# Encoder layer on one core: other slots, order and pieces for the expert weights, logits in column groups

## The chip, the cores and the metric

The kernel runs on one core of a Trainium2 chip. The metric is device time of one execution, in microseconds; the runs of the kernel before gave 1866.06, 1867.19 and 1870.11, so its median is 1867.19. A profiled execution of its own gave the trace that all rows below come from.

## The reference, cut to what matters

One encoder layer: 256 tokens of width 2048, float32. A token-mixing sub-layer (attention, a recurrent branch, gates, an output projection `w_out`) is followed by a routed mixture of 16 experts, in which each expert takes its own 32 best tokens.

```python
def expert_choice_ffn(hn, w_router, w_gate_e, w_up_e, w_down_e):
    cap = CAPACITY_FACTOR * T // N_EXPERTS                       # 32
    aff = softmax(hn @ w_router, axis=-1)                        # 256 tokens x 16 experts
    gate, idx = top_k(aff.transpose(0, 2, 1), cap)
    xe = hn[idx]                                                 # per expert 32 x 2048
    hid = silu(xe @ w_gate_e) * (xe @ w_up_e)                    # 2048 -> 1024
    ye = (hid @ w_down_e) * gate                                 # 1024 -> 2048
    return zeros.at[idx].add(ye)
...
h = h + merged @ w_out
h = h + expert_choice_ffn(rms_norm(h, ffn_norm_g), w_router, w_gate_e, w_up_e, w_down_e)
```

Every expert has three weight matrices of 8 MB, so the expert stage reads 384 MB of weights from HBM, each byte once.

## The kernel before, in words

The instructions of each engine stand in an order that a scheduler (the tile framework with a timeline simulation) chose; each engine then runs its own list in order, and waits on semaphores. DMAs are issued by SP, in order too: a DMA that has to wait holds up all that stand behind it on SP. Eight semaphores go round among SP's DMAs, and a DMA waits until the one eight places ahead has landed, so at most eight are in flight.

Stages: token mixing, to about 820 us of the trace; the output projection (`project_t`, tiles `pj_wo`), four blocks of 512 columns with eight chunks of weights each; routing; experts.

Output projection. `wsplit` (line 200) loads half a megabyte of weights into one of three buffers `raw`, splits it on ACT (`wh`) and DVE (`wl`), and PE runs 12 products on the chunk. Behind each block, PE transposes the finished columns of `h` and multiplies them with the router's weights (line 843, tile `plg`, eight products with 16 columns each); DVE adds the blocks' logits up in `lgt`.

Expert weights come in loads of 1 MB, `ew_loads`, in the order of use; `fetch` (line 171) issues the next one into a slot. There are 14 lasting slots (`NEW`, two of them in pool `ew1`, 12 in `ewa`), which are used round and round, and eight more (`NEB`, pool `ewb`), used once, in memory that becomes free when the output projection and its logits are done. `pace` (line 188) puts one load behind every third chunk (`PACE = 3`) of the last token-mixing blocks and of the output projection, until the 14 slots are full.

Routing (lines 855 to 893): softmax of the logits, then the 32 best tokens of each expert by four rounds of `max` and `match_replace` on DVE, and their places `slot`.

Experts are taken in four groups of four (`q`). `gather(k4)` (line 918) makes a quarter of the gathered, transposed tokens `xe` by products with a one-hot matrix `ohr` (PE, tile `pxe`, 16 records in the trace) and a multiplication on DVE. Eight steps `c` (line 928) use eight loads each (gate and up of four experts) and accumulate into four PSUM tiles `pgu`; the four experts stand in four groups of 32 columns of TensorE. Then the activation, transposes, and the down products (line 974, tile `pd`) in pieces of the 2048 output columns, given by `pieces`: two of 1024 columns, and in the last group one of 1024, one of 512 and two of 256. Behind each piece follow a copy on ACT (`ye`), products that scatter the rows back to the tokens (`poe`, line 982), an addition on DVE (`acc`), and in the last group the stores of `out`.

```python
NEW, NE1, NEB = 14, 2, 8
PACE = 3
...
for c in range(8):
    if c % 2 == 0:
        gather(c // 2)
    wt = []
    for j in range(4):
        wt += [expert_w(), expert_w()]
```

Of the kernel before, what the change touches and what calls it, by code (L numbers as in the profile page):

```python
# [8 lines left out]
F32 = mybir.dt.float32  # L9
# [9 lines left out]
T = 256  # L19
# [16 lines left out]
NEW, NE1, NEB = 14, 2, 8  # L36
PACE = 3
# [15 lines left out]
def trunk_kernel(ctx, tc, x, attn_norm_g, w_in, q_norm_g, k_norm_g, lambda_q1, lambda_k1, lambda_q2,  # L53
# [93 lines left out]
    def pieces(q):  # L147

        return ((0, 1024), (1024, 1024)) if q < 3 else ((0, 1024), (1024, 512), (1536, 256), (1792, 256))

    ew_loads = []
    for q in range(4):
        for c in range(8):
            for j in range(4):
                for src in (w_gate_e, w_up_e):
                    ew_loads.append(src[0, 4 * q + j].rearrange("(p kt) f -> p kt f", kt=KT)[:, 2 * c:2 * c + 2])
        for c0, w in pieces(q):
            n = 2048 // w
            for c in range(8 // n):
                for j in range(4):  # L160
                    ew_loads.append(w_down_e[0, 4 * q + j].rearrange("(p ft) n -> p ft n", ft=8)
                                    [:, n * c:n * c + n, c0:c0 + w])
    ew_state = dict(pools=[None, None, None], tiles=[], used=0, chunks=0)

    def slot_of(i):

        if NEW <= i < NEW + NEB:
            return 2
        return int((i if i < NEW else i - NEB) % NEW >= NE1)
# [30 lines left out]
    def wsplit(src, a, b, name):  # L200
        raw = wp.tile([128, 1024], F32, name="raw_" + name, tag="raw", bufs=3)
# [624 lines left out]
    with ExitStack() as es:  # L826
        o2 = es.enter_context(tc.tile_pool(name="out2", bufs=2, side=right))
        for blk in range(4):
# [32 lines left out]
    mx = rt_.tile([128, 6], F32, name="mx")  # L861
# [13 lines left out]
    V.tensor_copy(wk[0], paf)  # L875
    m8 = rt_.tile([16, 8], F32, name="m8")
    for i in range(4):
        a, b = wk[i % 2], wk[(i + 1) % 2]
# [9 lines left out]
    V.tensor_scalar(pos, pos, -1.0, None, op0=OP.add)  # L888
# [14 lines left out]
    with ExitStack() as es:  # L903
        ewb = tc.alloc_tile_pool(name="ewb", bufs=NEB, side=left)
        ew_state["pools"][2] = ewb
        for q in range(4):
# [11 lines left out]
            def gather(k4):  # L918
                px = mp.tile([128, 4, 128], F32, name=f"pxe{q}_{k4}", tag="x", bufs=1)
                for j in range(4):  # L920
                    kt = 4 * k4 + j
                    for t in range(2):
                        PE.matmul(px[:, j], h[:, t, kt::KT], ohr[:, t], start=t == 0, stop=t == 1)  # L923
                V.tensor_tensor(xe[k4], px,  # L924
                                fg[:, 4 * k4:4 * k4 + 4].unsqueeze(2).to_broadcast([128, 4, 128]), op=OP.mult)

            pgu = [pjp.tile([128, 512], F32, name=f"pgu{q}_{i}", tag="pj") for i in range(4)]
            for c in range(8):
                if c % 2 == 0:
                    gather(c // 2)  # L930
                wt = []
                for j in range(4):
                    wt += [expert_w(), expert_w()]
                for gu in range(2):
                    for k in range(2):
                        kt = 2 * c + k
                        for hf in range(2):
                            for j in range(4):
                                js = slice(32 * j, 32 * j + 32)
                                PE.matmul(pgu[2 * gu + hf][js], xe[kt // 4][:, kt % 4, js],  # L940
                                          wt[2 * j + gu][:, k, hf * 512:(hf + 1) * 512], start=kt == 0, stop=kt == KT - 1)
            if q == 0:
                ewb.release()
# [20 lines left out]
            for c0, cw in pieces(q):  # L964
                nw = min(cw, 512)
                nft = 2048 // cw
                pd = [misc([128, nw], f"pd{q}_{c0}_{i}") for i in range(cw // nw)]
                for c in range(8 // nft):
                    wt = [expert_w() for j in range(4)]
# [67 lines left out]
```

## Time and profile before

| what | value |
|---|---|
| median of 3 runs | 1867.19 us |
| profiled execution, its own time | 1860.5 us |
| its span, first to last instruction | 1858.7 us |
| PE busy | 1667.8 us, 90% |
| DVE, ACT, POOL busy | 700.0, 440.0, 197.0 us |
| moved by DMA | 556.48 MB, mean 299 GB/s |
| largest shares of the chain that ended last | PE 47%, DMA 38%, DVE 8% |

The busy shares are averages over stages with different limits: token mixing keeps PE, DVE and ACT busy and the DMA engines at half their time, the expert stage does the reverse. So the stage has to be read first, and the share second. "PE busy" says little in the expert stage, since a product that waits in the pipeline counts as busy.

### The profile page before, as it was taken

The numbers are of one execution on the slowest core, as the hardware profiler recorded it, in microseconds if no ns is written. First come the engines' busy times: TensorE is split into PE (matmuls) and PEld (weight loads), VectorE is DVE, ScalarE is ACT, GpSimd is POOL, SyncE is SP. The second block draws the span as 40 slices with busy tenths as digits, with TensorE's granted clock in tenths as the row PEclk, the third lists the DMA queues.
The fourth block names the chain that finished last, engine by engine and source line by source line (L and its number), as shares of the span: only waits on it lengthen the run. The fifth ranks groups of instructions, "written<-read, shape, count | busy, mean of one in ns | idle before, by whom it ended". The sixth has DMA issues, their size and how long they took to land.

```text
span 1858.7 us, 27458 instructions
## 1 busy us (share of the span) xinstructions
PE 1667.8 (90%) x11179; PEld 1024.7 (55%) x11179; DVE 700.0 (38%) x1523; ACT 440.0 (24%) x767; POOL 197.0 (11%) x304
## 2 busy tenths in 40 slices
PE   6999999999999999999799889888898888878878
PEld 5988888888997778998644222232222222211123
DVE  4687888787746778764500000000000000000000
ACT  6444444443434555444300000000000000000000
POOL 3243223333001321000000000000000000000000
PEclk9999999999999999999999999999999999999989
DMA  6545645455645666788899999999999999999997
GB/s 172 169 133 155 162 118 135 109 148 152 176 141 176 204 203 221 230 267 284 311 420 399 423 421 427 426 427 423 421 425 427 427 424 421 425 427 426 426 416 281
DMA packets 229598, 556.48 MB, mean 299 GB/s; under 512 B 40186, under 2 KB 137840, under 8 KB 196448
## 3 DMA queue, kind: packets, MB, share of 16 engines
q1 hardware_dynamic: 228896, 554.42, 79.7%
q8 instruction: 88, 1.44, 0.3%
q0 software_dynamic: 576, 0.31, 0.2%
q14 instruction: 38, 0.31, 0.0%
HBM read 543.14 MB, written 11.53 MB: 298 GB/s over the span
## 4 chain that ended last, share of the span: by engine, by line
PE 47%; DMA 38%; DVE 8%; POOL 3%; issue 2%; SPq 1%; ACT 1%; DVEq 0%; POOLq 0%; ACTq 0%
DMA w<-in_w_gate_e_dram 21%; DMA w<-in_w_down_e_dram 14%; PE pgu L940 8%; PE pd L974 2%; PE pc_gt L245 2%; PE pc_gt L247 2%; PE pc_gt L246 2%; PE pj_da L227 2%; PE pj_da L228 2%; PE pj_da L229 2%; PE pxe L923 2%; PE pc_br L245 2%; PE pc_br L247 2%; PE pc_br L246 2%; PE pj_wo L228 2%
## 5 line engine op out<-in xcount | busy, mean ns | idle before, releaser
L940 PE MATMUL pgu<-w,xe 128*32 128x512 f32 x2048 | 456.6, 607 | 64.2 <-DMA w<-in_w_gate_e_dram 33.0
L940 PEld LDWEIGHTS pgu<-w,xe 128*32 128x32 f32 x2048 | 110.9, 110 | 393.9 <-issue 232.6
L974 PE MATMUL pd<-w,hdT 128*32 128x512 f32 (+1 forms) x1088 | 246.2, 593 | 54.7 <-DMA w<-in_w_down_e_dram 53.8
L974 PEld LDWEIGHTS pd<-w,hdT 128*32 128x32 f32 x1088 | 64.7, 111 | 232.9 <-DMA w<-in_w_down_e_dram 122.1
L245 PE MATMUL pc_gt<-xh,wh_gt 128*128 128x256 f32 x512 | 148.4, 293 | 1.3 <-ACT wh_gt L207 1.3
L247 PE MATMUL pc_gt<-xh,wl_gt 128*128 128x256 f32 x512 | 142.9, 290 | 3.8 <-DVE wl_gt L208 3.5
L246 PE MATMUL pc_gt<-xl,wh_gt 128*128 128x256 f32 x512 | 144.5, 285 | 0.0
L955 ACT ACTIVATE th<-pgu 128x512 f32<-128x512 f32 x8 | 4.8, 597 | 521.4 <-PE pgu L940 521.4
L924 DVE TENSOR_TENSOR xe<-pxe,fg 128x512 f32<-128x512 f32 x16 | 11.0, 690 | 295.8 <-PE pgu L940 241.4
L245 PE MATMUL pc_rkv<-xh,wh_rkv 128*128 128x256 f32 x384 | 111.5, 293 | 2.3 <-ACT wh_rkv L207 1.7
L247 PE MATMUL pc_rkv<-xh,wl_rkv 128*128 128x256 f32 x384 | 109.3, 295 | 3.5 <-DVE wl_rkv L208 3.5
L246 PE MATMUL pc_rkv<-xl,wh_rkv 128*128 128x256 f32 x384 | 110.0, 289 | 0.0
L983 DVE TENSOR_TENSOR acc<-poe,acc 128x512 f32<-128x512 f32 (+1 forms) x26 | 16.9, 650 | 247.1 <-PE poe L982 247.0
L245 PEld LDWEIGHTS pc_gt<-xh,wh_gt 128*128 128x128 f32 x512 | 97.6, 191 | 4.6 <-ACT wh_gt L207 1.5
L956 DVE SCALAR_TENSOR_TENSOR th<-th,pgu 128x512 f32<-128x512 f32 x8 | 5.5, 687 | 249.7 <-ACT th L955 216.4
L247 PEld LDWEIGHTS pc_gt<-xh,wl_gt 128*128 128x128 f32 x512 | 95.0, 191 | 7.1 <-DVE wl_gt L208 4.6
L246 PEld LDWEIGHTS pc_gt<-xl,wh_gt 128*128 128x128 f32 x512 | 97.7, 191 | 2.0 <-issue 1.3
L208 DVE TENSOR_TENSOR wl_gt<-raw_gt,wh_gt 128x1024 fp32r<-128x1024 f32 x64 | 80.1, 1252 | 29.8 <-ACT wh_gt L207 27.7
L207 ACT CAST wh_gt<-raw_gt 128x1024 fp32r<-128x1024 f32 x64 | 66.9, 1046 | 80.4 <-PE pc_gt L246 62.6
L978 ACT COPY ye<-pd 128x512 f32<-128x512 f32 (+1 forms) x17 | 9.5, 560 | 309.7 <-PE pd L974 309.7
L228 PE MATMUL pj_da<-wl_da,xh 128*128 128x512 f32 x192 | 76.6, 399 | 1.7 <-DVE wl_da L208 1.7
L245 PEld LDWEIGHTS pc_rkv<-xh,wh_rkv 128*128 128x128 f32 x384 | 74.1, 193 | 6.0 <-ACT wh_rkv L207 2.2
(390 smaller groups left out, 2862.2 us busy)
## 6 DMA issues: line engine op xcount, KB each, us to landing
w<-in_w_gate_e_dram SPq DMA_DIRECT2D x128, 1024.0 KB, 19.5
w<-in_w_up_e_dram SPq DMA_DIRECT2D x128, 1024.0 KB, 19.5
w<-in_w_down_e_dram SPq DMA_DIRECT2D x128, 1024.0 KB, 18.1
raw_gt<-in_w_in_dram SPq DMA_DIRECT2D x64, 512.0 KB, 3.8
raw_rkv<-in_w_in_dram SPq DMA_DIRECT2D x48, 512.0 KB, 3.8
raw_da<-in_w_in_dram SPq DMA_DIRECT2D x48, 512.0 KB, 3.5
raw_wo<-in_w_out_dram SPq DMA_DIRECT2D x32, 512.0 KB, 5.6
raw_br<-in_w_branch_b_dram SPq DMA_DIRECT2D x16, 512.0 KB, 4.2
```

The costliest lines, as they stand in the source:

```text
L207: cast_ = A.copy(wh[:, :n], raw[:, :n])
L208: low_ = V.tensor_tensor(wl[:, :n], raw[:, :n], wh[:, :n].bitcast(F32), op=OP.subtract)
L227: PE.matmul(ps[t], lh[:, kt, s], wh[:, j], start=first, stop=False)
L228: PE.matmul(ps[t], lh[:, kt, s], wl[:, j], start=False, stop=False)
L229: PE.matmul(ps[t], ll[:, kt, s], wh[:, j], start=False, stop=last)
L245: PE.matmul(ps[c][:m], wh[:, j, cs], rh[:, kt], start=first, stop=False)
L246: PE.matmul(ps[c][:m], wh[:, j, cs], rl[:, kt], start=False, stop=False)
L247: PE.matmul(ps[c][:m], wl[:, j, cs], rh[:, kt], start=False, stop=last)
L923: PE.matmul(px[:, j], h[:, t, kt::KT], ohr[:, t], start=t == 0, stop=t == 1)
L940: PE.matmul(pgu[2 * gu + hf][js], xe[kt // 4][:, kt % 4, js], wt[2 * j + gu][:, k, hf * 512:(hf + 1) * 512], start=kt == 0, stop=kt == KT - 1)
L974: PE.matmul(pd[nb][js], hT[:, ft, js], wt[j][:, k, nb * nw:(nb + 1) * nw], start=ft == 0, stop=ft == 7)
L983: V.tensor_tensor(acc[:, t, cs], po, (h if q == 0 else acc)[:, t, cs], op=OP.add)
```

## The change

What it does, in the order of the program:

- Memory: the scratch for POOL's DMAs takes 2048 bytes a partition, `raw` has four buffers, `mx` is padded by 32 columns. The expert slots are 16 lasting ones and 6 + 2 that are used once, the last two in a pool of their own. In the built program all 24 slots start at multiples of 256 bytes; before, the 14 lasting ones did, and the eight others started 128 bytes past one.
- `PACE` is 2: one load behind every second chunk.
- Loads of gate and up weights: four gates, then four ups (before: gate, up, gate, up).
- Logits: per block four products, one in each group of 32 columns of TensorE, over 256 tokens, accumulated in PSUM over all blocks; at the end a copy on DVE and two products with a summing matrix `rsum`.
- Routing: two DVE instructions less (a copy, and a subtraction that moves into the constants).
- The first gather is made in two halves; the gathers of the later groups stand behind the products of the first four loads of the down stage of the group ahead (`issue_after(behind)`).
- The last 1024 columns of the last group: three chunks of the usual shape (two `ft`, 1024 columns, one expert a load), and then four loads that each hold one `ft` and 512 columns for all four experts, column half by column half; each half is scattered and stored when its two loads are used.

```diff
-NEW, NE1, NEB = 14, 2, 8
-PACE = 3
+NEW, NE1, NEB = 16, 2, (6, 2)
+PACE = 2
...
-            for j in range(4):
-                for src in (w_gate_e, w_up_e):
+            for src in (w_gate_e, w_up_e):
+                for j in range(4):
                     ew_loads.append(src[0, 4 * q + j].rearrange("(p kt) f -> p kt f", kt=KT)[:, 2 * c:2 * c + 2])
...
+            if last_piece(q, c0):
+                for nb in range(2):
+                    for ft in (6, 7):
+                        ew_loads.append(w_down_e[0, 4 * q:4 * q + 4].rearrange("e (p ft) n -> p e ft n", ft=8)
+                                        [:, :, ft, c0 + nb * 512:c0 + nb * 512 + 512])
...
-        raw = wp.tile([128, 1024], F32, name="raw_" + name, tag="raw", bufs=3)
+        raw = wp.tile([128, 1024], F32, name="raw_" + name, tag="raw", bufs=4)
...
-            pl = misc([128, 2, NE], f"plg{blk}")
-            for t in range(2):
-                for j in range(4):
-                    PE.matmul(pl[:, t], hT[:, j, t * 128:(t + 1) * 128], wr[:, blk * 4 + j], start=j == 0, stop=j == 3)
-            if blk == 0:
-                V.tensor_copy(lgt, pl)
-            else:
-                V.tensor_tensor(lgt, pl, lgt, op=OP.add)
+            for j in range(4):
+                PE.matmul(plg[32 * j:32 * j + NE], wr[:, blk * 4 + j], hT[:, j], start=blk == 0, stop=blk == 3)
+        lgs = o2.tile([128, T], F32, name="lgs", bufs=1)
+        V.tensor_copy(lgs, plg)
+        pl = misc([128, 2, NE], "pl")
+        for t in range(2):
+            PE.matmul(pl[:, t], lgs[:, t * 128:(t + 1) * 128], rsum[:, 0:NE], start=True, stop=True)
+        V.tensor_copy(lgt, pl)
...
-    V.tensor_copy(wk[0], paf)
...
-    V.tensor_scalar(pos, pos, -1.0, None, op0=OP.add)
...
-                if c % 2 == 0:
-                    gather(c // 2)
+                if q == 0 and c < 2:
+                    gather(0, c)
+                elif c % 2 == 0:
+                    with tc.issue_after(behind.ins) if q else nullcontext():
+                        gather(c // 2)
...
+                for ft in range(6 if last_piece(q, c0) else 8):
+                    if ft % 2 == 0:
+                        wt = [expert_w() for j in range(4)]
+                    for nb in range(2):
+                        mm = down(nb, ft, [w[:, ft % 2, nb * 512:(nb + 1) * 512] for w in wt])
+                    if c0 == 0 and ft == 1:
+                        behind = mm
+                for nb in range(2):
+                    if last_piece(q, c0):
+                        for ft in (6, 7):
+                            w4 = expert_w()
+                            down(nb, ft, [w4[:, j] for j in range(4)])
+                    scatter(nb)
```

Three places show how the lists of the engines change. First SP at the end of the output projection (`raw_wo` are its weights, `w` the expert loads), before:

```order
L205 DMA raw_wo_4_10745<-in_w_out_dram 128x2x512
L205 DMA raw_wo_5_10763<-in_w_out_dram 128x2x512
L179 DMA w<-in_w_gate_e_dram 128x2048
L205 DMA raw_wo_6_10784<-in_w_out_dram 128x2x512
L205 DMA raw_wo_7_10802<-in_w_out_dram 128x2x512
L179 DMA w<-in_w_gate_e_dram 128x2048
L179 DMA w<-in_w_up_e_dram 128x2048 x2
L179 DMA w<-in_w_gate_e_dram 128x2048
L179 DMA w<-in_w_up_e_dram 128x2048
```

and now:

```order
L209 DMA raw_wo_4_10746<-in_w_out_dram 128x2x512
L209 DMA raw_wo_5_10764<-in_w_out_dram 128x2x512
L183 DMA w<-in_w_up_e_dram 128x2048
L209 DMA raw_wo_6_10782<-in_w_out_dram 128x2x512
L209 DMA raw_wo_7_10800<-in_w_out_dram 128x2x512
L183 DMA w<-in_w_up_e_dram 128x2048
L183 DMA w<-in_w_gate_e_dram 128x2048 x4
L183 DMA w<-in_w_up_e_dram 128x2048 x4
```

The load behind `raw_wo_7` is the 16th now, where it was the 12th; the rows behind it are the loads into the slots that are used once. Their first waits now for the last product of the output projection (`pj_wo`) alone, and the seventh for the logits; before, the first waited for the last `plg` product, and with it all eight.

Then PE in the first group of experts, from the transposes `phd` on (`pd` are the down products, `pxe` the gathers of the next group), now:

```order
L974 MATMUL phd_1_11355<-cst,hd 128x128 x4
L982 MATMUL pd_0_0_11361<-w,hdT 32x512 x2
L982 MATMUL pd_0_1_11362<-w,hdT 32x512 x2
...
L982 MATMUL pd_0_1_11362<-w,hdT 32x512 x4
L933 MATMUL pxe_0_11602<-ohr,h 128x128 x8
...
L933 MATMUL pxe_1_11708<-ohr,h 128x128 x8
L982 MATMUL pd_0_0_11361<-w,hdT 32x512
L982 MATMUL pd_0_1_11362<-w,hdT 32x512
L933 MATMUL pxe_2_11814<-ohr,h 128x128 x8
...
L933 MATMUL pxe_3_11920<-ohr,h 128x128 x8
```

Before, three of these four gathers stood among the gate and up products of the group ahead, and none behind `phd`:

```order
L940 MATMUL pgu_1_10937<-w,xe_10935 32x512
L923 MATMUL pxe_3_11926<-ohr,h 128x128 x8
L940 MATMUL pgu_0_10936<-w,xe_10935 32x512
...
L962 MATMUL phd_1_11361<-cst,hd 128x128 x4
L974 MATMUL pd_0_0_11367<-w,hdT 32x512
L974 MATMUL pd_0_1_11368<-w,hdT 32x512
```

Last, the end of PE's list (the last 1024 columns of the last group), before:

```order
L974 MATMUL pd_1024_0_13556<-w,hdT 32x512 x32
L982 MATMUL poe_1024_0_0_13607<-ye,gT 128x512
L982 MATMUL poe_1024_0_1_13610<-ye,gT 128x512
L974 MATMUL pd_1536_0_13615<-w,hdT 32x256 x32
L982 MATMUL poe_1536_0_0_13658<-ye,gT 128x256
L982 MATMUL poe_1536_0_1_13661<-ye,gT 128x256
L974 MATMUL pd_1792_0_13666<-w,hdT 32x256 x32
L982 MATMUL poe_1792_0_0_13709<-ye,gT 128x256
L982 MATMUL poe_1792_0_1_13712<-ye,gT 128x256
```

and now:

```order
L982 MATMUL pd_1024_0_13550<-w,hdT 32x512 x8
L991 MATMUL poe_1024_0_0_13638<-ye,gT 128x512
L991 MATMUL poe_1024_0_1_13642<-ye,gT 128x512
L982 MATMUL pd_1024_1_13551<-w,hdT 32x512 x8
L991 MATMUL poe_1024_1_0_13660<-ye,gT 128x512
L991 MATMUL poe_1024_1_1_13664<-ye,gT 128x512
```

Of the 32 products that stood between two scatters eight are left; the others come earlier, as their loads land. On SP the store of the first 1024 columns, which stood ahead of the last two loads, now stands behind all of them.

## Rows read from the trace of the kernel before

**Rows 1.** The page: GB/s moved in each of 40 equal slices of the span.
```profile
GB/s 172 169 133 155 162 118 135 109 148 152 176 141 176 204 203 221 230 267 284 311 420 399 423 421 427 426 427 423 421 425 427 427 424 421 425 427 426 426 416 281
```

**Rows 2.** Windows: us, engines' busy time (instructions), PEclk, DMA share, GB/s.
```profile
824.00:910.00 86.00, 86.00 (x415) 71.87 (x414) 38.60 (x38) 37.04 (x47) 1.57 (x9) 1.00 0.84 294
910.00:915.00 5.00, 4.87 (x25) 3.63 (x24) 2.20 (x3) 1.06 (x3) 0.30 (x1) 1.00 0.71 301
915.00:920.00 5.00, 2.43 (x19) 2.00 (x17) 2.48 (x17) 2.21 (x8) 0.00 (x0) 1.00 0.31 100
920.00:935.00 15.00, 6.55 (x34) 4.72 (x38) 8.61 (x26) 0.00 (x0) 0.00 (x0) 0.54 1.01 425
950.00:990.00 40.00, 39.22 (x203) 21.28 (x202) 4.21 (x7) 0.37 (x1) 0.00 (x0) 1.00 1.01 426
995.00:1005.00 10.00, 10.00 (x64) 3.12 (x62) 0.00 (x0) 0.00 (x0) 0.00 (x0) 1.00 0.75 298
1130.00:1280.00 150.00, 131.30 (x546) 43.17 (x545) 6.02 (x10) 1.54 (x3) 0.00 (x0) 0.97 1.01 427
1290.00:1365.00 75.00, 62.19 (x252) 16.16 (x252) 3.21 (x5) 2.24 (x4) 0.00 (x0) 1.00 1.03 421
1802.00:1820.00 18.00, 13.25 (x54) 3.35 (x49) 2.77 (x4) 1.17 (x2) 0.00 (x0) 0.94 1.05 405
1844.00:1848.00 4.00, 4.00 (x27) 2.21 (x27) 0.00 (x0) 0.00 (x0) 0.00 (x0) 1.00 0.43 152
```

**Rows 3.** Timeline of SP: start, us, DMA issues (expert loads, one store).
```profile
903.62 2.30 SPq L179 DMA_DIRECT2D w<-in_w_up_e_dram  x2
917.53 0.33 SPq L179 DMA_DIRECT2D w<-in_w_gate_e_dram  x1
...
937.40 0.80 SPq L179 DMA_DIRECT2D w<-in_w_gate_e_dram  x2
...
985.27 0.38 SPq L179 DMA_DIRECT2D w<-in_w_up_e_dram  x1
1000.16 0.33 SPq L179 DMA_DIRECT2D w<-in_w_gate_e_dram  x1
...
1829.36 3.24 SPq L986 DMA_DIRECT2D out_dram<-acc  x2
```

**Rows 4.** Tile w, the expert weights: products' weight loads, and issue to landing.
```profile
L940 PEld LDWEIGHTS pgu<-w,xe x2048: 106/110/178, 933.7 to 1764.2; 128*32 128x32 f32 x187
...
DMA to landing us min/median/max: 4.5/18.8/21.1
```

**Rows 5.** Timeline of PE, end of the output projection to the first experts.
```profile
896.02 1.86 PE L843 MATMUL plg<-wr,hT 128*128 128x16 f32 x16
...
913.47 0.39 PE L229 MATMUL pj_wo<-wh_wo,ml 128*128 128x512 f32 x1
...
929.04 3.84 PE L923 MATMUL pxe<-ohr,h 128*128 128x128 f32 x16 [1.20 <-DVE ohr L913]
...
933.67 2.85 PE L940 MATMUL pgu<-w,xe 128*32 128x512 f32 x24 [0.36 <-DVE xe L924]
```

**Rows 6.** Timeline of DVE in routing: the two instructions that go.
```profile
921.22 0.41 DVE L875 COPY wk<-paf 16x256 f32<-16x256 f32 x1 [0.69 <-PE paf L872]
...
927.05 0.28 DVE L888 TENSOR_SCALAR wk<-wk 16x256 f32<-16x256 f32 x1
```

**Rows 7.** The chain that ended last, its end: start, us, what.
```profile
1800.43 3.62 PE pd L974 x20
...
1826.61 0.59 ACT ye L978
...
1829.23 11.45 PE pd L974 x64
...
1842.31 11.45 PE pd L974 x64
...
1855.42 0.42 DVE acc L983
```

More of the change, by code (lines that the diff above doesn't have):

```diff
@@ L1 @@
 import math
-from contextlib import ExitStack, contextmanager
+from contextlib import ExitStack, contextmanager, nullcontext
 import concourse.bass as bass
@@ L145, in trunk_kernel, with last_piece @@
                 V.scalar_tensor_tensor(xl[:, kt], pt[:, i], g, xh[:, kt].bitcast(F32), op0=OP.mult, op1=OP.subtract)
-    def pieces(q):
-        return ((0, 1024), (1024, 1024)) if q < 3 else ((0, 1024), (1024, 512), (1536, 256), (1792, 256))
+    def last_piece(q, c0):
+        return q == 3 and c0 > 0
     ew_loads = []
@@ L963, in trunk_kernel, with down, scatter @@
                 A.copy(hT[:, 4 * f4:4 * f4 + 4], pt)
[L964 to L969, printed above, removed]
-                    for k, nb, j in ([(k, 0, j) for j in range(4) for k in range(nft)] if nft == 8 else
-                                     [(k, nb, j) for k in range(nft) for nb in range(cw // nw) for j in range(4)]):
-                                ft = nft * c + k
-                                js = slice(32 * j, 32 * j + 32)
-                                PE.matmul(pd[nb][js], hT[:, ft, js], wt[j][:, k, nb * nw:(nb + 1) * nw],
-                                          start=ft == 0, stop=ft == 7)
-                for nb in range(cw // nw):
+            for c0 in (0, 1024):
+                pd = [misc([128, 512], f"pd{q}_{c0}_{i}") for i in range(2)]
+                def down(nb, ft, wf):
+                    for j in range(4):
+                        js = slice(32 * j, 32 * j + 32)
+                        mm = PE.matmul(pd[nb][js], hT[:, ft, js], wf[j], start=ft == 0, stop=ft == 7)
+                    return mm
+                def scatter(nb):
@@ L983, in trunk_kernel @@
                         V.tensor_tensor(acc[:, t, cs], po, (h if q == 0 else acc)[:, t, cs], op=OP.add)
-                if q == 3:
+                        if last_piece(q, c0):
+                            SP.dma_start(out[0, t * 128:(t + 1) * 128, cs], acc[:, t, cs])
+                for ft in range(6 if last_piece(q, c0) else 8):
+                    if ft % 2 == 0:
+                        wt = [expert_w() for j in range(4)]
+                    for nb in range(2):
+                        mm = down(nb, ft, [w[:, ft % 2, nb * 512:(nb + 1) * 512] for w in wt])
+                    if c0 == 0 and ft == 1:
+                        behind = mm
@@ L985, in trunk_kernel @@
+                for nb in range(2):
+                    if last_piece(q, c0):
+                        for ft in (6, 7):
+                            w4 = expert_w()
+                            down(nb, ft, [w4[:, j] for j in range(4)])
+                    scatter(nb)
+                if q == 3 and c0 == 0:
                     for t in range(2):
-                        SP.dma_start(out[0, t * 128:(t + 1) * 128, c0:c0 + cw], acc[:, t, c0:c0 + cw])
+                        SP.dma_start(out[0, t * 128:(t + 1) * 128, 0:1024], acc[:, t, 0:1024])
```

62 lines of the change are left out of this document (33 added, 29 removed).

## The prediction

> **What bounds the kernel now.** I read the page's slices first: up to slice 20 the kernel moves a good half of what it moves afterwards, and from slice 21 on 420 to 427 GB/s almost without a gap [rows 1]. So the program has two halves with different limits, and a line by line ranking over the whole span would mix them. Windows by stage come next [rows 2]. In the output projection (824 to 910 us) PE is busy for all of 86.00 us, with the DMA engines at 0.84: PE sets the time. From 920 us on the DMA share is 1.01 to 1.05, while PE has idle time (131.30 of 150 in 1130 to 1280): in the expert stage the weights set the time. One load of 1 MB (1.0486 MB) takes 1.0486/427 = 2.46 us among gate and up loads, 1.0486/421 = 2.49 us among down loads with 4 KB runs, and 1.0486/405 = 2.59 us with 2 KB runs [rows 2].
>
> A stage that DMA bounds is shortened only by starting its stream earlier, closing its gaps, making its loads quicker, or shortening what follows the last byte. The timeline of SP and the low windows give the gaps: 915 to 920 with 100 GB/s and 995 to 1005 with 298 [rows 2, 3]. In 1844 to 1848 the share is 0.43; against 1.05 at full rate, that is 1.6 us of data, so the last byte lands near 1845.6 and the span, 1858.7, ends 13.1 us later. The end of the chain shows what fills these [rows 7].
>
> **The change part by part.** The sum is made against the profiled execution's own 1860.5 us, which is 6.7 below the median of the runs; that difference is added at the end.
>
> *1. Logits.* A block's `plg` is 16 records in 1.86 us [rows 5]. Now it is four products, eight records of 256 columns. The lower bound is the weight load alone, 8 x 0.110 = 0.9 us [rows 4]; the upper is 11.45/64 = 0.179 a record of 256 columns [rows 7], so 1.4. I take 1.1: 0.75 less for each of the three blocks that stand inside dense PE work, 2.3 us in all (1.3 to 2.9). The fourth stands behind the projection's last product. That product ends at 913.47 + 0.39 = 913.9 [rows 5], and now at 911.6.
>
> *2. Start of the stream.* The first load into a once-used slot goes out at 917.53 [rows 3], because it waits for the last `plg`. In 915 to 920 the engines are nearly empty. Now it waits for the last projection product, so 911.7, and 16 loads instead of 14 are there or under way. What is late next is the first reuse of a slot. The first expert product is at 933.67, 19.8 us after the projection's last [rows 5]. Of that path go 0.41 and 0.28 on DVE [rows 6], about 0.4 by half a first gather (half of the 3.84 us, most of it beside other work), and some 0.5 is added by the copy `lgs` and the two summing products: 19.2, with 0 to 1 for the addition. The first `pgu` product is then at 930.8. The first slot came free 937.40 - 933.67 = 3.7 us after it [rows 3, 5]; now 934.5. A load on unloaded engines lands after 4.5 us [rows 4], so the 25th lands at 939.0. Before, it was the 11th after 917.53: 917.53 + 4.5 + 10 x 2.47 = 946.7 (425 GB/s). Gain 7.7, with 5 to 10 as bounds. Supply alone would give more, since the 24 loads are there by about 911.7 + 9 x 2.47 = 934, half a microsecond before the slot; so the routing path, not the stream, sets this.
>
> *3. The gap at 995 to 1005.* No load is issued between 985.27 and 1000.16 [rows 3], because three gathers of the next group stand among the gate and up products and hold the slots. The window moves 298 instead of 426 GB/s: 10 x (1 - 298/426) = 3.0 us at most, 10 x (1.01 - 0.75) = 2.6 by the share, and nothing if the pause only comes back at another place. I take 2, nearer to the row. The gathers now stand behind the first `pd` products: 4 x 3.84 = 15.4 us of PE time [rows 5], some 19 us with the products in between. In that time 19/2.49 = 8 loads land. There are 16 slots and at most eight loads in flight, so eight landings are covered; the stage then has PE time to catch up (62.19 busy of 75 in 1290 to 1365 [rows 2]). I cost it at nothing; what it costs without that cover is rival E.
>
> *4. The last 16 loads.* Before, they were eight with 2 KB runs and eight with 1 KB, and the store of `out` (1 MB) was issued at 1829.36, ahead of the last two [rows 3]. They took from about 1800.4, where the last products on the loads before them begin [rows 7], to 1845.6: 45.2 us. Now it is 12 x 2.49 + 4 x 2.59 = 40.2, and the store comes behind them: gain 5.0.
>
> The four new loads fetch four runs per partition, 8 MB apart; no row shows such a load. From below, 2.46 us each [rows 2] (0.1 less each). From above, the slowest stretch of the stream, 100 GB/s in 915 to 920, though that was starved and not slow: 10.5 each, 32 more in all. I take 2.59, the row with runs of the same size, since all loads of the trace fetch runs spread over 128 partitions and their rate moves with the size of a run by some per cent only. The Trainium skill ("DMA: Bandwidth & Descriptors", section "Latency and other measured facts") reports that rows a large power of two apart drop to 103 GB/s at 8 MiB. By that a load takes 10.2 us as an estimate, and the sum gives a loss of about 10. In these four loads 128 partitions lie as close as before and only four runs of each are far apart, so I weigh the rule as rival F.
>
> *5. The tail.* Before, two pieces of 64 `pd` records of 11.45 us each stand behind one another at the end, the last from 1842.31 to 1853.8 [rows 7]. Now four products, one copy, two `poe`, an addition and the store follow the last byte. By the gather's 3.84/16 = 0.24 for 128 columns [rows 5], 512 columns take 0.96; with the weight load, 1.15. Copy 0.59; two `poe` 2.0; addition 0.75 (0.42 for half of the columns, `acc` [rows 7]); the store 1858.7 - 1855.84 = 2.9 before, with twice the bytes 3.2. Sum 7.7 against 13.1: gain 5.4. If TensorE runs at the lower of its two levels there, as it did in 920 to 935 (mean 0.54 [rows 2]), the products cost up to 3.1 more.
>
> *6. At nothing.* A fourth `raw` buffer lies where PE is dense; -1 to +4, should it lift a wait for a chunk that the 86 busy us hide. The smaller scratch for POOL: 0, POOL is idle in the expert stage [rows 2]. The order of gates and ups: 0, the bytes are the same. Multiples of 256: the once-used slots, 128 bytes off, were filled in 920 to 935 at 425 GB/s, the aligned ones in 950 to 990 at 426 [rows 2]: 0. The Trainium skill (same page, section "How a descriptor splits into AXI transactions") lets a run that starts off a 256-byte boundary cost extra beats. Where it holds for writes that is at most some 2% of eight loads by an estimate from the page, 0.3 us, and the two rows agree with nothing.
>
> Sum: 2.3 + 7.7 + 2 + 5.0 + 5.4 = 22.4, but 1 and 2 share: the 2.3 us by which the projection ends earlier are inside the 7.7 already. That leaves 20.1. The profiled execution would take 1840.4, the median of the runs 1847.
>
> **The rivals.**
> *A, the forecast*: 1841 to 1852.
> *B, more*: the fourth buffer or a wait I have not seen gives 6 us beyond the sum: below 1841. For it: PE's busy time counts a waiting product too; against it, nothing in the rows shows such a wait.
> *C, the projection becomes bound by DMA, or the tail is slow.* The 32 chunks take 86 us [rows 2], two of them 5.4. In these, with `PACE` 2, two chunks (0.52 MB each) and one load go by, 2.1 MB: 390 GB/s, where 294/0.84 = 350 is what the engines did at full share there. If they hold 350 over the 28 chunks that carry 14 loads (75 us), 75 x (390/350 - 1) = 8.6 us are lost. Against it: from 920 on they do 425 on loads alone, and before and behind the paced chunks there is slack. With a part of that, or the 3.1 of part 5: 1852 to 1859.
> *D, nothing comes of it, the change doesn't do what it says*: the 25th load is as late as before because routing grows by what it saves, and the store or scatter of the last two halves fills the tail: 1860 to 1871. Parts 4 and 5 would both have to fail; the end of the chain speaks against it.
> *E, slower*: the gathers in the down stage starve the engines. They hold PE for 15.4 us before the second half of the products can free slots. If the covering slots are four and not eight, 19 - 4 x 2.49 = 9 us a stage are lost, in three stages 27: 1847 + 27 = 1874. It decides at about 7 us a stage, where the 20 are gone. For it: three gathers of the same kind did make the gap at 985 to 1000 [rows 3]. Against it: there 14 slots, eight of them once-used before, and one row of gate and up products holds eight loads, a row of down products four.
> *F, the four mixed loads are slow*: at 5.2 us each (twice the 2.59) the loss is 10, so 1857; at the skill's rate above it would be 1877 by an estimate. The change loses from 2.59 + 20/4 = 7.6 us a load.
>
> **How the numbers follow.** A 0.62, B 0.05, C 0.18, D 0.05, E 0.06, F 0.04. The forecast is A's middle, 1847. Its bounds and the cases next to it, C and the mild end of F, make the range 1839 to 1860; it leaves out D, E and half of B and F. A measurement of this kernel can tell 0.2%, 3.7 us, from no change. Faster: A, B, C and half of F, less a few for what I can't see: 0.86. Same: most of D, 0.05. Slower: E, half of F and the rest, 0.09.
>
> **What would show it.** Part 1: `plg` as eight records of about 1.1 us, and the projection's last product at 911 to 912. Part 2: first once-used load issued within 1 us of that product, no window under 300 GB/s from 912 to 934, first `pgu` at 930 to 931.5, the 25th load landed at about 939. Part 3: no gap in SP's issues over 5 us between 950 and 1000, and in each down stage a DMA share of 1.0 through the gathers; a share under 0.9 there is rival E. Part 4: the last four loads 2.6 us apart; 5 or more is F. Part 5: the span ends 7 to 8 us after the last landing, with the granted clock at 1.00. A projection that ends after 914, with waits of PE on `raw` or `wh`, is rival C. If PE runs without idle time from 950 to 1800 while the DMA share falls below 1, the reading of the whole stage as DMA-bound is wrong.

## The result and the profile after

The changed kernel takes 1843.22 us (median of 4, 1838.98 to 1844.11) against 1866.62 us of the kernel before: a ratio of 0.9877, 95% interval 0.9856 to 0.9898. 1847 was forecast, 1839 to 1860 the range. The profiled execution has a span of 1836.9 us, before 1858.7: 21.8 less.

The page of the profile after, GB/s in 40 slices (answers to [rows 1]):

```profile
GB/s 184 164 141 152 169 120 127 120 139 154 175 141 181 195 209 204 225 271 363 294 390 427 423 420 426 427 427 424 421 425 427 427 425 420 425 426 427 426 420 358
```

The picture is the old one, a slow first half and a stream at 420 to 427 behind it; the last slice has risen from 281 to 358. Windows of the profile after, with the columns of [rows 2]:

```profile
824.00:910.00 86.00, 85.89 (x407) 69.20 (x405) 40.24 (x37) 36.96 (x47) 2.59 (x14) 1.00 0.89 326
910.00:915.00 5.00, 2.31 (x18) 1.30 (x16) 2.90 (x18) 1.91 (x7) 0.00 (x0) 0.83 0.92 341
915.00:920.00 5.00, 0.59 (x2) 0.12 (x2) 3.22 (x12) 0.85 (x4) 0.00 (x0) 0.50 1.01 426
920.00:935.00 15.00, 11.15 (x72) 6.00 (x76) 5.00 (x13) 0.00 (x0) 0.00 (x0) 0.65 0.80 320
931.00:934.00 3.00, 3.00 (x32) 0.85 (x28) 0.00 (x0) 0.00 (x0) 0.00 (x0) 1.00 0.00 0
995.00:1005.00 10.00, 8.21 (x32) 1.91 (x32) 0.00 (x0) 0.00 (x0) 0.00 (x0) 1.00 1.01 428
1301.00:1320.00 19.00, 19.00 (x111) 9.02 (x112) 3.46 (x5) 1.17 (x2) 0.00 (x0) 1.00 1.03 420
```

The hole at 915 to 920 is gone (426 instead of 100 GB/s), and 995 to 1005 is full (428 instead of 298). But a hole as large stands in 920 to 935: 320 instead of some 426 GB/s over 15 us are 3.7 us of data, where 100 over 5 us were 3.8, and from 931 to 934 nothing moves at all. It comes behind 24 landed loads, where the old one came behind 14. In the last row PE makes gathers all the while, without an idle moment, and the DMA engines stay at 1.03: the forecast's slower case, gathers that starve the stream, doesn't happen.

The timeline of SP in the profile after (start, us, issues; answers to [rows 3]):

```profile
909.44 2.04 SPq L183 DMA_DIRECT2D w<-in_w_gate_e_dram  x4
911.52 3.32 SPq L183 DMA_DIRECT2D w<-in_w_up_e_dram  x4
933.05 1.97 SPq L183 DMA_DIRECT2D w<-in_w_gate_e_dram  x4
936.49 1.77 SPq L183 DMA_DIRECT2D w<-in_w_up_e_dram  x4
```

The timeline of PE (answers to [rows 5]):

```profile
892.69 0.62 PE L850 MATMUL plg<-hT,wr 128*16 128x256 f32 x8
...
909.02 0.39 PE L233 MATMUL pj_wo<-wh_wo,ml 128*128 128x512 f32 x1
...
924.21 2.12 PE L933 MATMUL pxe0h<-ohr,h 128*128 128x128 f32 x8 [1.20 <-DVE ohr L920]
926.12 1.97 PE L933 MATMUL pxe<-ohr,h 128*128 128x128 f32 x8
...
928.45 14.88 PE L951 MATMUL pgu<-w,xe 128*32 128x512 f32 x128
```

The once-used loads go out 0.03 us behind the projection's last product. Reuse of slots starts at 933.05, 1.7 us behind the landing of the 24th load (931.38). And the end of the program, all engines (answers to [rows 7]):

```profile
1828.91 1.06 PE L982 MATMUL pd<-w,hdT 128*32 128x512 f32 x8 [0.31 <-DMA w<-in_w_down_e_dram]
1830.09 0.59 ACT L987 COPY ye<-pd 128x512 f32<-128x512 f32 x1 [4.53 <-PE pd L982]
...
1830.73 1.98 PE L991 MATMUL poe<-ye,gT 128*128 128x512 f32 x4 [0.76 <-ACT ye L987]
...
1832.75 0.69 DVE L992 TENSOR_TENSOR acc<-poe,acc 128x512 f32<-128x512 f32 x1 [0.17 <-PE poe L991]
```

The last eight records wait for the last load and for nothing else; before, 64 records of 11.45 us stood there, twice.

**One ruler for all runs.** Spans of single executions can't be compared to 5 us: the stretch ahead of the output projection (the same work everywhere) ended between 817.1 and 825.2 us in these profiles, so each execution is measured in pieces from landmarks. The table gives, in us: the projection, first to last `pj_wo` product; from there to the landing of the 25th expert load; from that to the landing of the 368th; the last 16 loads; from the last landing to the end of the span; and the sum of the last four. A load's landing is its DMA's completion in the trace.

| run | projection | to 25th load | 25th to 368th | last 16 | tail | sum of four |
|---|---|---|---|---|---|---|
| before | 95.75 | 34.38 | 852.14 | 44.92 | 13.38 | 944.8 |
| after | 92.34 | 28.32 | 850.95 | 40.18 | 8.03 | 927.5 |
| again (e12) | 92.35 | 27.20 | 851.07 | 40.15 | 8.03 | 926.5 |
| logits as before (e1) | 95.44 | 27.15 | 851.08 | 40.16 | 8.03 | 926.4 |
| 14 slots (e2) | 92.37 | 31.90 | 851.22 | 42.78 | 8.03 | 933.9 |
| gathers ahead (e3) | 92.31 | 27.15 | 850.99 | 40.29 | 8.03 | 926.5 |
| one pool (e4) | 92.35 | 30.20 | 849.78 | 40.15 | 8.02 | 928.2 |
| slots 128 bytes off (e5) | 92.33 | 27.17 | 866.29 | 41.16 | 8.05 | 942.7 |
| four pieces (e6) | 92.34 | 27.05 | 851.02 | 42.28 | 16.06 | 936.4 |
| usual last loads (e7) | 92.35 | 27.20 | 851.18 | 39.85 | 11.73 | 930.0 |
| gate, up in turn (e8) | 92.36 | 26.91 | 850.99 | 40.18 | 8.04 | 926.1 |
| slots 64 bytes off (e9) | 92.35 | 27.71 | 866.63 | 41.32 | 8.06 | 943.7 |
| stream as before (e10) | 92.38 | 31.71 | 851.95 | 43.10 | 9.34 | 936.1 |
| fine tail (e11) | 92.38 | 27.15 | 850.86 | 40.31 | 6.82 | 925.1 |

Before against again: 3.4 + 7.2 + 1.1 + 4.8 + 5.4 = 21.8 us with unrounded terms, from the projection's start to the end.

### The profile page after: what moved, and what is told of

Read it like the earlier page. It is cut to its first block, busy times and chain, and to the rows that moved or that the text cites. A ratio compares the mean times of both kernels' runs of the same rounds, so it can differ in the third digit from the quotient of the medians.

```text
span 1836.9 us, 27260 instructions
## 1 busy us (share of the span) xinstructions
PE 1652.7 (90%) x11083; PEld 1012.1 (55%) x11083; DVE 701.4 (38%) x1520; ACT 440.2 (24%) x766; POOL 199.2 (11%) x308
## 4 chain that ended last, share of the span: by engine, by line
DMA 45%; PE 40%; DVE 7%; POOL 3%; issue 2%; SPq 1%; ACT 1%; DVEq 0%; POOLq 0%; ACTq 0%
DMA w<-in_w_gate_e_dram 22%; DMA w<-in_w_down_e_dram 13%; DMA w<-in_w_up_e_dram 9%; PE pd L982 2%; PE pc_gt L251 2%; PE pc_gt L249 2%; PE pc_gt L250 2%; PE pxe L933 2%; PE pj_da L231 2%; PE pj_da L232 2%; PE pj_da L233 2%; PE pc_rkv L249 2%; PE pc_br L249 2%; PE pc_rkv L251 2%; PE pc_rkv L250 2%
## 5 line engine op out<-in xcount | busy, mean ns | idle before, releaser
L951 PE MATMUL pgu<-w,xe 128*32 128x512 f32 x2048 | 473.9, 600 | 86.4 <-DMA w<-in_w_up_e_dram 44.6
L982 PE MATMUL pd<-w,hdT 128*32 128x512 f32 x1024 | 217.1, 598 | 32.7 <-DMA w<-in_w_down_e_dram 31.8
L982 PEld LDWEIGHTS pd<-w,hdT 128*32 128x32 f32 x1024 | 54.0, 109 | 182.7 <-issue 90.4
L992 DVE TENSOR_TENSOR acc<-poe,acc 128x512 f32<-128x512 f32 x24 | 16.6, 692 | 175.9 <-PE poe L991 175.9
L987 ACT COPY ye<-pd 128x512 f32<-128x512 f32 x16 | 9.4, 586 | 301.1 <-PE pd L982 301.1
L251 PEld LDWEIGHTS pc_rkv<-xh,wl_rkv 128*128 128x128 f32 x384 | 73.5, 196 | 5.1 <-DVE wl_rkv L212 2.8
```

The source lines that it names most:

```text
L251: PE.matmul(ps[c][:m], wl[:, j, cs], rh[:, kt], start=False, stop=last)
L982: mm = PE.matmul(pd[nb][js], hT[:, ft, js], wf[j], start=ft == 0, stop=ft == 7)
L992: V.tensor_tensor(acc[:, t, cs], po, (h if q == 0 else acc)[:, t, cs], op=OP.add)
```

## The experiments

The theory: the expert stage is a stream of loads, and the gain is made of independent pieces, nearly all of them at its two ends. Each run undoes one part of the change, so that a piece must come back alone; rivals say that another part or nothing pays for it. The ratios are to the kernel before, with their 95% intervals.

**e1, the logits as before**

```diff
-            for j in range(4):
-                PE.matmul(plg[32 * j:32 * j + NE], wr[:, blk * 4 + j], hT[:, j], start=blk == 0, stop=blk == 3)
+            pl = misc([128, 2, NE], f"plg{blk}")
+            for t in range(2):
+                for j in range(4):
+                    PE.matmul(pl[:, t], hT[:, j, t * 128:(t + 1) * 128], wr[:, blk * 4 + j], start=j == 0, stop=j == 3)
```

> The changed kernel with the logits of before (per block eight products of 16 columns, added up by DVE); all else as changed. Compared with the changed kernel (span 1836.9, projection's last product over at 909.4, first pgu 928.45, 25th load landed 937.73). Theory: the projection is dense PE work and the routing path behind it sets the first reuse of a slot, so what the logits take passes through to the end. plg takes 1.86 us per block against 0.62, three blocks stand in dense work: the projection ends 3.7 us later, near 913.1, the 25th load lands 3 to 4 us later, the span is 1840 to 1841.5. Rival 1: the fourth raw buffer made the projection shorter, not the logits: it ends within 1 us of 909.4 and the span stays within 1 us. Rival 2: the start of the stream is set by supply: the projection ends later, but the 25th load stays at 938.

Timeline of PE, inside the dense projection:

```profile
901.45 1.86 PE L848 MATMUL plg<-wr,hT 128*128 128x16 f32 x16
903.15 0.48 PE L232 MATMUL pj_wo<-wl_wo,mh 128*128 128x512 f32 x1
```

The second line is the projection, which goes on at once behind `plg`: what `plg` takes, it loses. It takes 95.44 instead of 92.35, 3.1 us for three blocks, and nothing else in the run's row of the table moves. The theory holds; the other 0.3 against before (95.75) belongs to the fourth `raw` buffer, the pace and the rest of the change together. Ratio to before 0.9895 (0.9867 to 0.9923).

**e2, 14 lasting slots**: `NEW, NE1, NEB = 14, 2, (6, 2)`.

> The changed kernel with 14 lasting slots instead of 16 (22 loads ahead of the first reuse instead of 24). Theory: the first reuse is set by routing at 933.05 and the engines run dry before it, so two loads fewer are there at that time and everything behind lands 2 x 2.45 = 4.9 us later: span 1841 to 1843, more only if the gathers in the down stages are no longer covered. Rival 1: the start is set by the supply of the stream: the number of slots does not matter, span within 1 us. Rival 2: the slots are what covers the gathers: with 14 the engines starve there, a DMA share under 0.95 in the windows of the gathers of three down stages, 3 us or more each, span 1850 or more.

Timeline of SP, the start and the end:

```profile
910.96 0.82 SPq L183 DMA_DIRECT2D w<-in_w_up_e_dram  x2
911.82 2.15 SPq L183 DMA_DIRECT2D w<-in_w_gate_e_dram  x4
914.27 19.81 SPq L183 DMA_DIRECT2D w<-in_w_up_e_dram  x4
...
1815.43 6.20 SPq L1011 DMA_DIRECT2D out_dram<-acc  x2
1821.72 2.98 SPq L183 DMA_DIRECT2D w<-in_w_down_e_dram  x2
```

The 23rd load, in the third row, waits until 933 for a slot; the 25th load lands 31.90 behind the projection, 4.7 later than in e12: two loads, as the theory says. The other 2.6 us lie in the last 16 loads: with fewer slots the scheduler put the 1 MB store ahead of the last two loads again. The gathers stay covered (420 GB/s in 1300 to 1325). Ratio 0.9925 (0.9898 to 0.9951).

**e3, the gathers ahead**: `with nullcontext():` in place of `with tc.issue_after(behind.ins) if q else nullcontext():`.

> The changed kernel with the gathers of the later groups placed by the scheduler again (they stand among the gate and up products of the group ahead). Theory: they hold the slots there and a pause of SP's issues as that at 985 to 1000 in the kernel before returns, with a low window: 1 to 3 us in all, span 1838 to 1840. Rival 1: with 16 slots and gates before ups the slots cover them there too: the span stays within 0.7 us. Rival 2: the pauses of all three groups count: 6 us or more.

The window where the kernel before paused:

```profile
985.00:1000.00 15.00, 15.00 (x83) 9.34 (x85) 0.85 (x2) 0.00 (x0) 0.00 (x0) 1.00 1.01 426
```

PE is just as busy with gathers there, and the stream runs at 426. 850.99 and 926.5 are the changed kernel's own values: the first rival. Where the gathers stand is worth nothing once there are 16 slots and the gates come first. Ratio 0.9877 (0.9853 to 0.9900).

**e4, the eight once-used slots in one pool**: `NEW, NE1, NEB = 16, 2, (8,)`.

> The changed kernel with the eight once-used slots in one pool, so that the first of them waits for the logits' last product too, as before, and not for the projection's last alone. Theory: the first once-used load is issued near 914 instead of 909.4, the 24th lands near 935.5 instead of 931.4; the first reuse of a slot at 933.05 comes from the routing path and is unchanged, so the 25th load lands at most 1.5 us later than 937.73: span 1836.9 to 1838.4. Rival: the start of the stream sets all that follows: 4.5 us, span 1841 or more.

```profile
921.27 2.04 SPq L183 DMA_DIRECT2D w<-in_w_gate_e_dram  x4
923.36 2.00 SPq L183 DMA_DIRECT2D w<-in_w_up_e_dram  x4
939.34 2.39 SPq L183 DMA_DIRECT2D w<-in_w_gate_e_dram  x4
```

(SP.) The projection ended at 916.88; its first once-used load is 4.4 us late, the first reuse comes 22.5 us behind the projection, as in e12 (940.07 - 917.57). The 25th load is 3.0 late against e12, twice the bound of 1.5, of which 1.3 return before the 368th: a late landing (3.4 to 4.1 us behind the one ahead, where 2.45 is usual) of the kind that every profile has every 100 to 120 loads fell ahead of the 25th here. Net 1.7 us for 4.4 us of delay. The theory's mechanism holds, its bound was low. What goes ahead of the late landings can be seen in the traces: each stands 2 to 4 us behind the start of a packet of 16 KB of the queue that the profile calls instruction, which takes 0.9 to 1.1 us, and in the steady stream it is every eighth of these packets. Why only every eighth is not shown. Ratio 0.9888 (0.9857 to 0.9919).

**e5, all slots 128 bytes off**

```diff
-    mx = rt_.tile([128, 6 + 32], F32, name="mx")
+    mx = rt_.tile([128, 6 + 64], F32, name="mx")
+    hres.tile([128, 32], F32, name="pad")
     ew1 = tc.alloc_tile_pool(name="ew1", bufs=NE1, side=right)
```

> The changed kernel with all 24 expert slots (and the output's tile) 128 bytes past a multiple of 256, by 128 bytes of padding on each side; nothing else moved. Theory: the start of a slot is of no account, as the once-used slots of the kernel before filled at 425 GB/s: gate and up loads 2.44 us apart, 427 GB/s, span within 1.5 us of 1836.9. Rival: each run of 4 KB that starts off a 256-byte boundary costs one more transfer of 128 bytes, 4 beats on 128 or 1.6 to 3%: loads 2.48 to 2.52 us apart, 360 loads x 0.04 to 0.08 = 14 to 28 us, span 1850 to 1865.

Windows of a gate and up stage and of a down stage:

```profile
1130.00:1280.00 150.00, 124.44 (x491) 29.38 (x490) 4.04 (x7) 1.57 (x3) 0.00 (x0) 1.00 1.01 421
1290.00:1365.00 75.00, 67.92 (x304) 27.23 (x300) 5.54 (x8) 1.17 (x2) 0.00 (x0) 1.00 1.03 410
```

The same stages in e12, with aligned slots:

```profile
1130.00:1250.00 120.00, 100.84 (x396) 23.71 (x394) 2.56 (x5) 0.37 (x1) 0.00 (x0) 0.99 1.01 427
1300.00:1340.00 40.00, 37.62 (x189) 17.64 (x192) 4.83 (x7) 1.17 (x2) 0.00 (x0) 1.00 1.03 421
```

421 and 410 GB/s instead of 427 and 421, at the same share: the engines are as busy and bring less. Between the 25th and the end the run loses 16.2 us, and the ratio is 0.9984 (0.9970 to 0.9999): an offset of 128 bytes undoes nearly the whole change. The theory falls, the rival stands.

**e6, the last 1024 columns in pieces of 512, 256 and 256** (the loads and loops of before for them).

> The changed kernel with the last 1024 columns as before (pieces of 512, 256 and 256 columns, loads with runs of 2 KB and 1 KB, the store of the first 1024 columns where the scheduler puts it). Theory: the last 16 loads take 45 us instead of 40.2 and the tail behind the last landing 13.4 instead of 8.0: span 1836.9 + 4.8 + 5.4 = 1847. Rival 1: the tail was hidden elsewhere and the new one only ends in other waits: within 3 us. Rival 2: the two parts overlap (a late tail has its loads early): 5 us.

Timeline of PE, the end:

```profile
1821.65 10.83 PE L982 MATMUL pd<-w,hdT 128*32 128x256 f32 x61
1833.00 1.13 PE L992 MATMUL poe<-ye,gT 128*128 128x256 f32 x4 [0.52 <-ACT ye L988]
1834.06 11.50 PE L982 MATMUL pd<-w,hdT 128*32 128x256 f32 x64
1846.07 1.13 PE L992 MATMUL poe<-ye,gT 128*128 128x256 f32 x4 [0.52 <-ACT ye L988]
```

42.28 + 16.06 = 58.3 us for the last 16 loads and the tail, as before (44.92 + 13.38 = 58.3), and 10.2 more than the changed kernel. But here no store stands ahead of the last loads: they land 2.6 us sooner and the tail is 2.7 us longer. PE's two blocks of 64 records set the end, not the loads. Ratio 0.9929 (0.9907 to 0.9951).

**e7, the last four loads in the usual shape** (four chunks instead of three and the mixed loads).

> The changed kernel with the last four loads in the usual shape too (one expert each, two row tiles, 1024 columns), then both halves scattered and stored; it tells what the four mixed loads give. Theory: the four loads land 4 x 0.05 to 0.1 us sooner, but behind the last landing stand 16 products instead of 4 and two scatters instead of one: 16 x 0.12 = 1.9 to 3.7 us of products instead of 1.1, and a second scatter of some 2 us beside the copy: tail 11 to 13 us instead of 8.0, span 1839 to 1841.5. Rival: mixed loads are slow and eat what they give: span within 1 us or below.

```profile
1833.19 3.62 PE L977 MATMUL pd<-w,hdT 128*32 128x512 f32 x20 [0.58 <-DMA w<-in_w_down_e_dram]
...
1836.74 3.70 PE L986 MATMUL poe<-ye,gT 128*128 128x512 f32 x8
```

Behind the last load stand 3.6 us of products and two scatters: tail 11.73. The mixed loads give 3.7 there and cost 0.3 in landing. The theory holds. Ratio 0.9901 (0.9880 to 0.9921).

**e8, gate and up in turn** (the loops over `src` and `j` exchanged, eight loads taken at once).

> The changed kernel with gate and up loads in turn, as before, instead of four gates and then four ups. Theory: 16 products then need the first, third, fifth and seventh load, and slots come free in that order while SP fills them in order: the second reuse waits for the ups' products, so SP's first issues come 4 and 4 with a wait of 3.7 us between single loads; in the steady state DMA is the bound and the order is of no account. First reuse at 933 as now; loss 0 to 3 us, all of it before 960 us, span 1836.9 to 1840. Rival: the order matters in every step, since PE starts a step only when seven loads are there instead of four: low windows all through the stage, 5 us or more.

926.1 against 926.5 in e12 and no piece that differs by more than 0.3: the order of gates and ups is of no account here. Ratio 0.9872 (0.9848 to 0.9896).

**e9, all slots 64 bytes off**: the padding of e5 with 48 columns in both places.

> The changed kernel with all 24 expert slots 64 bytes past a multiple of 256 (128 bytes cost 1.7% of a gate or up load, 2.485 against 2.444 us, and 3.0% of a down load, 2.560 against 2.486, some 16 us in all). Theory A: what counts is the bytes between the boundary below and the start, which are fetched or written as well: 64 bytes cost half of it, 2.465 and 2.523 us a load, 8 us in all from the projection's end. Theory B: what counts is that the run needs one transfer more, whatever its size: as with 128 bytes, 2.485 and 2.560, 16 us. Theory C: the 128 bytes hit something else (two halves of one port): nothing or more than 16.

```profile
1130.00:1280.00 150.00, 124.20 (x492) 29.41 (x491) 4.03 (x7) 1.57 (x3) 0.00 (x0) 1.00 1.01 421
1290.00:1365.00 75.00, 68.47 (x308) 27.52 (x308) 5.53 (x8) 1.51 (x3) 0.00 (x0) 1.00 1.03 410
```

The rates of e5: theory B. The packets of the trace say it more finely. A gate or up load moves in packets of 8 KB, a down load in packets of 4 KB; their mean times are 309.4 and 159.1 ns in e12, 313.8 and 163.6 in e5, 313.9 and 163.5 in e9. The kernel before has 309.4 and 159.1 too, with its lasting slots aligned at other addresses, so it is not the shift as such. Each packet costs 4.4 ns more, whatever its size and whichever of the two offsets. Eight 8 KB packets on each of 16 engines give 35 ns a load, sixteen of 4 KB 70: the median intervals between landings grew by 41 and 74. (In the first loads behind a pause the packets read 309 ns in e5 and e9 too, but the loads land 2.46 to 2.49 us apart there already, where the changed kernel has 2.44 to 2.46: the interval is the safer measure.) Ratio 0.9989 (0.9974 to 1.0004).

**e10, 14 slots, gathers ahead, gate and up in turn**: e2, e3 and e8 together.

> The changed kernel with 14 lasting slots, the gathers placed by the scheduler and gate and up loads in turn: all three parts of the stream as before together, where 14 slots alone cost 4.9 us at the start and the two others nothing. Theory: the pause before needs all of it: few slots, held by gathers ahead. Beside the 4.9 us at the start (25th load 31.9 us behind the projection's end), a window near 995 to 1005 with about 300 GB/s, and 2 to 3 us more between the 25th and the 368th load: 853 to 854 instead of 851. Rival: the pause had another cause (the once-used slots' release, the third raw buffer): 851 to 851.5.

```profile
995.00:1005.00 10.00, 10.00 (x63) 3.14 (x64) 0.00 (x0) 0.00 (x0) 0.00 (x0) 1.00 0.87 345
```

The low window is there again, where e3 had none, but it is less deep (345, before 298: 1.9 us of data missing instead of 3.0), and 0.9 us are lost between the 25th and the 368th load, not 2 to 3. Mechanism as in the theory, size below it; whether the slots need both the gathers' place and the order of gates and ups beside them, no run shows. The 4.5 us at the start and 2.9 for the store are as in e2. The tail is 1.3 longer because the last `poe` took 3.29 us instead of 1.98, at a granted clock of 0.76 in 1843 to 1848 (1.00 in 1829 to 1834 of the profile after). Ratio 0.9945 (0.9927 to 0.9962).

**e11, a finer tail**: the last 512 columns in two PSUM tiles of 256; both halves of the products, then `scatter(1, 0, 256)` and `scatter(1, 256, 256)`.

> The changed kernel with the last 512 columns in two halves of 256 behind the last loads: products, copy, scatter, addition and store of 256 columns each. Theory: the last landing is unchanged; behind it stand 0.6 us of products for each half, a copy of 0.35, the second half's copy and scatter beside the first's, an addition of 0.4 and the store: tail 6.2 to 6.6 us instead of 8.03, span 1.5 us less from the projection's end (925 instead of 926.4). Rival: 256 columns a product are no quicker where the weight load counts (64 records took 11.45 us in the kernel before), and the four small stores go one after the other on SP: tail 8 us or more.

```profile
1832.17 1.07 PE L987 MATMUL pd<-w,hdT 128*32 128x256 f32 x16 [0.31 <-DMA w<-in_w_down_e_dram]
1832.93 0.80 ACT L993 COPY ye<-pd 128x256 f32<-128x256 f32 x2 [4.11 <-PE pd L987]
...
1833.36 1.99 PE L997 MATMUL poe<-ye,gT 128*128 128x256 f32 x8
1834.09 1.72 DVE L998 TENSOR_TENSOR acc<-poe,acc 128x256 f32<-128x256 f32 x4 [2.50 <-PE poe L997]
```

Sixteen records of 256 columns take what eight of 512 did, 1.07, but copy, scatter and addition now overlap: tail 6.82 instead of 8.03, a little above the 6.2 to 6.6 expected. By the ruler it is the fastest of all, 1.3 us below e12. By times, 0.9871 (0.9853 to 0.9888) against 0.9895 (0.9880 to 0.9910) for e12 on the same chip, the intervals overlap, so the times alone don't show it.

**e12, the changed kernel again.**

> The changed kernel itself once more, to see what differs between executions of one program. Theory: the stretch ahead of the output projection takes 817 to 825 us from one execution to the next, whatever the kernel, and all behind it repeats: projection 92.3 us, 25th load 27 to 28.5 us behind its end, 851.0 to the 368th, 40.2 for the last 16, tail 8.03. Rival: the 1.1 us by which the projection started earlier in the changed kernel is of the change: 817 again.

The projection began at 825.22, not 817, and everything behind it repeats within 0.2, but for the 25th load (27.20; 28.32 in the first profile). So of the 21.8 us between the first two spans 1.05 were the earlier start of one execution, and the start of the stream was 1.1 slower in it than elsewhere. Ratio 0.9895 (0.9880 to 0.9910).

## Why the prediction was right, and where its steps were not

The forecast of 20.1 us less stands beside 21.8 by the ruler. The limits were read rightly: two ends of a stream, each with its own wait. That the sum came within 1.7 us is in part luck: part 2 was 2.9 too low and part 3 0.9 too high. Undone one by one, the logits (3.1), two slots (4.7 at the start), the two pools (1.7) and the last pieces (10.2), with 1.1 for the gap, make 20.8 of the 21.8; that they simply add was not tried. By the steps:

- *Part 1, logits*: 2.3 forecast, 3.1 by e1. Eight records take 0.62 us, below the lower bound of 0.9. The bound multiplied the weight loads of 32 columns (0.110), one behind another; those of 16 columns take 92 to 96 ns, and the four products in four column groups overlap: in the trace four records of 0.39 us each start within 0.02 us. Before, each of the 16 records loaded 128 columns of weights (186 to 193 ns) and started 0.11 behind the one ahead; no run parts the groups from the smaller weights.
- *Part 2, start of the stream*: with the projection's part 7.7 forecast, 3.4 + 7.2 = 10.6 measured. Two steps failed by size: the 1.1 of the projection, and 1.5 in the kernel before, whose 25th load was put at 32.8 us behind the projection and landed at 34.4. The landings there, to the 25th, were 2.41 to 2.72 us apart, 2.49 in the mean, where 2.47 was used, and one was a late one of 3.7. The step that mattered held: reuse of a slot sets the 25th load. 27.4 behind the projection's end were forecast, 27.2 measured in e12 (28.3 in the first profile, where the first slot came free 4.6 us behind the first `pgu`, in e12 3.7), and two more slots are worth 4.7 (e2), which part 2 had inside its difference and did not price. One sign failed: no window under 300 GB/s was to stand between 912 and 934, and from 931 to 934 nothing moved. The 24 loads were there 1.7 us ahead of the slot (0.4 in e12, half a microsecond forecast), and the load that then goes out lands 4.7 us later, so such a hole follows from the forecast's own numbers.
- *Part 3, the gap*: 2 forecast, 1.1 measured, and the cause was told too simply. The low window of the kernel before lacks 3.0 us of data, as the forecast read, but the load that lands in it, the 47th, is only 1.6 late. Gathers among the gate and up products don't stop the stream (e3); gathers with only 14 slots and alternating gates do (e10, 0.9 of it). The cover of eight landings that the forecast counted for the new place holds at the old place too.
- *Part 4, last 16 loads*: 5.0 forecast, 4.8 measured; *part 5, tail*: 5.4 and 5.4. The sum of 10.4 is right, the split was not: the forecast left some 2.5 of part 4, what smaller runs don't explain, to the store ahead of the last loads, and e6 has the store behind them and gains nothing. In the kernel before the store was hidden behind PE's blocks; what paid is the shape of the pieces. Where the tail is short, as in e2 and e10, the same store does cost 2.6 to 2.9.
- *Rival F*: the four mixed loads land 2.48 to 2.57 us apart in the profile after. Of the slow rate that the Trainium skill gives for copies of rows at a large power of two ("DMA: Bandwidth & Descriptors", section "Latency and other measured facts") nothing is seen where runs of one partition lie 8 MB apart and 128 partitions 64 KB. *Rival E*: share 1.03 through the gathers. *Rival C*: the projection was not slowed by the faster pace: with the logits as before, and four `raw` buffers, it takes 95.44 us (e1), in the kernel before 95.75.
- *Part 6, alignment at nothing*: right for the eight slots that the change aligns (some 0.3 us at 41 ns a load), wrong as a reading. "The two rows agree with nothing" compared two windows, 425 and 426 GB/s, one of which held six loads. The landings in the same trace told it: into the slots off the boundary the 16th to the 19th load came 2.47 to 2.50 us apart, into the aligned ones behind them the 23rd to the 25th 2.41 to 2.45. e5 has 421 against 427 in 150 us. The Trainium skill's rule (same page, section "How a descriptor splits into AXI transactions") was right that a start off 256 bytes costs; the page tells it of what is read, and here the side that is written is off. By an estimate from that page 128 bytes are four beats more, 1.6% of 8 KB and 3.1% of 4 KB, where the median intervals grew by 1.7 and 3.0%. By it 64 bytes should cost half, and e9 costs as much as e5, so for the size the measurement decides. With all 24 slots off the boundary, 16 of the 21.8 us would have been lost again (e5).

## What to carry to other kernels

Where a stream of DMAs bounds a stage, count what lies ahead of its first reuse of a buffer and behind its last byte, and undo parts one at a time: the parts that look alike (gathers, order, store) may be worth nothing once another part has given slack (e3, e8). Measure from landmarks inside the trace when the stretch ahead varies by more than what is sought. And look at the start address of every buffer of a long stream: 128 bytes cost 1.7 to 3% of it here.

## What had not been expected of the hardware

- A packet that starts 64 or 128 bytes past a multiple of 256 in SBUF takes 4.4 ns longer in the steady stream, whether it has 4 KB (159.1 to 163.6 ns) or 8 KB (309.4 to 313.8); other offsets were not tried. On a stream that is at 1.01 to 1.03 share all of it is time: 16.2 us in e5.
- Four products with 16 weight columns each in four column groups, 256 columns of data: 0.62 us for all eight records, where 16 records with 128 weight columns and 16 columns of data, one after another, took 1.86.
- A packet of 16 KB of the instruction queue, 0.9 to 1.1 us long, goes ahead of every late landing of the stream (see e4); each such landing comes 1 to 1.6 us late.
- The granted clock at the end differs between profiles: the last scatter took 1.98 us in most and 3.29 in e10 (mean 0.76 in 1843 to 1848, behind 1.00 in 1838 to 1843 with PE busy for 2.39 of 5 us). In e2, where the same store delays the last loads, it took 1.98 again, so the cause is open.
